# Two low parts of the first attention tile and one norm factor's power, issued later

## Chip, core and metric

The kernel runs on one core of a Trainium2 chip. The metric is device time in microseconds of one execution. Before the change three runs gave 1406.76, 1407.80 and 1407.81 us; the median is 1407.8.

## What is computed

The reference is one encoder block on a sequence of 1024 tokens of width 1024, with 16 meta tokens ahead of them. Two attention branches work on the same normalised input; their outputs are gated and merged, and a feed-forward block follows. The change is in branch A, which is differential attention:

```python
s1 = einsum(q1, k1) * scale + bias
s2 = einsum(q2, k2) * scale + bias
attn = softmax(s1) - lam * softmax(s2)
y = rms_norm(attn @ v, subln_g) * (1 - lambda_init)
...
merged = sigmoid(ga) * (y_a @ w_ba) + sigmoid(gb) * (y_b @ w_bb)
```

`ga` and `gb` are the gate projections of the input. All products are in fp32 precision: each factor is split into a high part (rounded to fp32r) and a low part (what the rounding left), and three fp32r products are added.

## The kernel before

Branch A has 4 heads of 8 tiles of 128 queries. For a tile, `scores_a` (line 1070 on) runs through the two softmaxes, m = 1 and then m = 0. For each, TensorE writes the first 704 keys to a double PSUM bank `two`, of which there is one, and the last 336 keys to a bank of the tag `sc`, of which there are three (line 1091). VectorE adds the bias and finds the row's extreme with one instruction for each part, lines 1094 and 1098; since signs are turned, it is a minimum, `amn`. Each is followed by a short instruction that reads the minimum out, and line 1098 starts from the minimum of line 1094. ScalarE takes the exponential and its sum (line 1102). After m = 0, VectorE works out the factor of the two sums (1107) and combines both softmaxes (1108, the "combine", 1040 columns).

One tile later, `transpose_a` turns the combined tile on TensorE in three blocks of 4, 4 and 1 pieces (line 1121), each into a bank `sc`. For each block ScalarE writes the high part (1124) and VectorE the low part (1125) to the tile `at`, which the value products (1134) read after two tiles.

After four tiles, `normed_a` makes the norm factors `af`: sums on TensorE (1147), a small VectorE step (1152), and on GpSimd a power of -1/2 on 128x4 numbers (1153). Some steps later TensorE spreads the factor (1158).

The products of branch A leave VectorE and ScalarE much to do, so the gate projections run in between on TensorE: `gate_steps` issues them in quarters of three products each (line 980). They use a Strassen scheme, so GpSimd first adds and subtracts weight blocks (lines 857, 858, 864 and others), then writes the high part (876, a cast) and the low part (877) of a gate weight `wopg`. Four of these exist at a time. A quarter's first two products need the high part, the third the low part.

The order on TensorE is the order of the code, set by the lists `SLOTS`, and GpSimd's is so at the start of branch A. On the other engines and queues a scheduler sets the order at build time from a simulated timeline; `tc.issue_after(x)` keeps what is issued under it behind instruction x. Each engine then works through its list in order.

Of the kernel before, what the change touches and what calls it, by code (L numbers as in the profile page):

```python
# [14 lines left out]
ALU = mybir.AluOpType  # L15
# [64 lines left out]
def encoder_block(ctx: ExitStack, tc: tile.TileContext, x, meta, norm_mix, w_in, lq1, lk1, lq2, lk2,  # L80
                  subln, sink, w_ba, w_bb, w_o, norm_ffn, w_g, w_u, w_d, norm_final, out, dbg=None):
    nc = tc.nc
# [5 lines left out]
    def f32(ap):  # L88
        return ap.bitcast(F32)
# [13 lines left out]
    def bank(p, tag, name, bufs):  # L103
        return p.tile([P, 512], F32, tag=tag, name=name, bufs=bufs)
# [15 lines left out]
    neg_half = const.tile([P, 4], F32, name="neg_half")  # L120
# [67 lines left out]
    def pp_bank(name):  # L188
        i = turn_pp[0] % 3
        turn_pp[0] += 1  # L190
        return bank(psum1, "pp", name, 1) if i == 2 else bank(psumg, f"pp{i}", name, 1)
# [339 lines left out]
    def turn_x(t, lows=None):  # L531
        parts = P if t < NT else NM
        return transposed(lambda name: bank(psum1, ("bt", "bs")[t % 2], name, 2), xns.pop(t), parts, hT_hi, hT_lo, t * P, f"a{t}", lows)
# [23 lines left out]
    pt = bank(psum1, "bt", "gain_t", 2)  # L557
# [3 lines left out]
    for b in range(2):  # L561
        pt = pp_bank(f"gain_{b}")
        gain.append(pt)
        for c in range(4):
            k = 4 * b + c
# [18 lines left out]
    low = normals[-1]  # L584
    for i in (0, 2, 1, 3):
        with tc.issue_after(low.ins):
            low = lows[i]()
# [28 lines left out]
    third, low, turned = turn_x(2)  # L616
# [5 lines left out]
    highs, low, turned = turn_x(3)  # L622
# [26 lines left out]
    _, low, _ = turn_x(NT)  # L649
# [189 lines left out]
    sums_g, keys_a, raws_g, values_in, turned_t, made_g = {}, [], [], [], {}, []  # L839
# [198 lines left out]
    def far_copy(n):  # L1038
        if n < AH * NT:
            with ExitStack() as after:  # L1040
                if n > 2:
                    after.enter_context(tc.issue_after(made_g[-1].ins))
                nc.gpsimd.tensor_copy(far_m[n % 3][:, 0:S - 704], dist[:, 1600 - n % NT * P:1600 - n % NT * P + S - 704])
# [30 lines left out]
    def scores_a(h, t, ld, s):  # L1074
        slope = 2.0 ** -(2 * (h + 1))
        qs, ks, _ = ld
        nm = f"{h}_{t}"
        mn = small.tile([P, 2, 4], F32, tag="amn", name=f"amn_{nm}")
        dn = small.tile([P, 2], F32, tag="adn", name=f"adn_{nm}")
        if t % 4 == 0:  # L1080
            sum_a[h, t // 4] = small.tile([P, 4], F32, tag="asum", name=f"asum_{nm}")
        first_sum = sum_a[h, t // 4][:, t % 4:t % 4 + 1]
        u0 = 896 - t * P
        far = far_m[(h * NT + t) % 3]
        for m in (1, 0):
            s[m] = s0s[t % 2] if m == 0 else apool.tile([P, L], F32, tag="s1", name=f"as1_{nm}", bufs=S_BUFS[1])
            two = psum2.tile([P, 2, 512], F32, tag="two", name=f"aps2_{nm}_{m}", bufs=1)
            for i, (k0, n) in enumerate(A_CHUNKS):
                ps = two[:, i] if i < 2 else bank(psum2, "sc", f"aps_{nm}_{m}", SC)
                for vv in range(2):  # L1090
                    nc.tensor.matmul(ps[:, :n], qs[m][:, t * P:(t + 1) * P], ks[m][:, vv, k0:k0 + n],  # L1091
                                     start=(vv == 0), stop=(vv == 1))
                if i == 1:
                    nc.vector.tensor_tensor_reduce(s[m][:, 0:2 * n].rearrange("p (a k) -> p a k", a=2), two[:, :, :n],  # L1094
                                                   dist[:, u0:u0 + 2 * n].rearrange("p (a k) -> p a k", a=2), slope, far_a,
                                                   ALU.add, ALU.min, mn[:, m, 0:1])
                elif i == 2:
                    nc.vector.tensor_tensor_reduce(s[m][:, k0:k0 + n], ps[:, :n], far, slope, mn[:, m, 0:1],  # L1098
                                                   ALU.add, ALU.min, mn[:, m, 1:2])
                if i < 2:  # L1100
                    yield
            nc.scalar.activation(s[m][:, 0:L], s[m][:, 0:L], AF.Exp, bias=mn[:, m, 1:2], scale=-1.0,  # L1102
                                 accum_out=dn[:, 1:2] if m else first_sum)
            if m:
                nc.vector.reciprocal(dn[:, 1:2], dn[:, 1:2])
            yield
        nc.vector.tensor_scalar(dn[:, 0:1], first_sum, dn[:, 1:2], neglam, ALU.mult, ALU.mult)
        nc.vector.scalar_tensor_tensor(s[0][:, 0:L], s[1][:, 0:L], dn[:, 0:1], s[0][:, 0:L], ALU.mult, ALU.add)
        more, last = s[0][:, L:L + 2 * NM].rearrange("p (a k) -> p a k", a=2), s[0][:, S:L].unsqueeze(1).broadcast_to([P, 2, NM])
        nc.scalar.copy(more, last)  # L1110
        far_copy(h * NT + t + 2)

    def transpose_a(h, t, s, at_):
        i = t % 2
        for b in range(3):
            nb = 4 if b < 2 else 1
            kp = P
            pt = bank(psum2, "sc", f"apt_{h}_{t}_{b}", SC).rearrange("p (k t) -> p k t", k=4)
            for j in range(nb):
                k = 4 * b + j  # L1120
                nc.tensor.transpose(pt[:kp, j, :], s[:, k * P:k * P + kp], ident)  # L1121
            hi = at_[:kp, 4 * b:4 * b + nb, 0, i * P:(i + 1) * P]
            lo = at_[:, 4 * b:4 * b + nb, 1, i * P:(i + 1) * P] if b < 2 else hi[:NM]
            nc.scalar.activation(hi, pt[:kp, :nb], AF.Copy)
            nc.vector.tensor_tensor(lo, pt[:lo.shape[0], :nb], f32(hi)[:lo.shape[0]], ALU.subtract)
            yield

    def values_a(h, t, v, at_, py):
# [9 lines left out]
    def normed_a(h, c, py):  # L1138
        nm = f"{h}_{c}"
        ysq = gwork.tile([P, 512], F32, tag="ysq", name=f"ysq_{nm}", bufs=1)  # L1140
        nc.scalar.activation(ysq, py, AF.Square)
        yg = ustage.tile([P, 512], F32, tag="yg", name=f"yg_{nm}", bufs=2)
        nc.scalar.activation(yg, py, AF.Copy, scale=gsub)
        yield
        pst = bank(psum2, "sc", f"apst_{nm}", SC)
        for i in range(4):
            nc.tensor.matmul(pst[:, i:i + 1], ysq[:, i * P:(i + 1) * P], ones, start=True, stop=True)
        f = small.tile([P, 4], F32, tag="af", name=f"af_{nm}", bufs=2)
        sums = sum_a.pop((h, c))
        e = small.tile([P, 4], F32, tag="ae", name=f"ae_{nm}", bufs=2)  # L1150
        nc.vector.scalar_tensor_tensor(e, sums, EPS, sums, ALU.mult, ALU.mult)
        nc.vector.scalar_tensor_tensor(f, pst[:, 0:4], 1.0 / P, e, ALU.mult, ALU.add)
        nc.gpsimd.tensor_tensor(f, f, neg_half, ALU.pow)
        for _ in range(N_WAIT):
            yield
        pf = bank(psum2, "sc", f"apf_{nm}", SC)
        for i in range(4):
            nc.tensor.transpose(pf[:, i * P:(i + 1) * P], f[:, i:i + 1].broadcast_to([P, P]), ident)
        nc.vector.tensor_tensor(yg, yg, pf, ALU.mult)
        nc.sync.dma_start(ya_d[h][:, c * 512:c * 512 + 512], yg)  # L1160
        yield
# [14 lines left out]
    def turn(done):  # L1176
        h, t, s, at_, v = done
        yield from transpose_a(h, t, s[0], at_)

    def later(done):  # L1180
        h, t, s, at_, v = done
        if t % 4 == 1:
            acc[0] = bank(psum2, "acc", f"apy_{h}_{t}", 1)
        yield from values_a(h, t, v, at_, acc[0])
        if (h, t) == (AH - 1, NT - 1):
            valued.append(t)
        if t % 4 == 3:
            yield from normed_a(h, t // 4, acc[0])
# [11 lines left out]
    for n in range(AH * NT + T_LAG):  # L1200
# [3 lines left out]
        if n < AH * NT:  # L1204
            h, t = divmod(n, NT)
# [23 lines left out]
            s = [None, None]  # L1229
# [382 lines left out]
    xns, sums_t, held = {}, {}, {}  # L1612
# [315 lines left out]
    for n in range(nf, len(steps)):  # L1928
        p, j = steps[n][1]
# [6 lines left out]
        if p in LOADS:  # L1936
            at, half, col = LOADS[p]
            if at <= j < at + 4:
                t, cols = 4 * half + j - at, slice(col * 512, col * 512 + 512)
# [63 lines left out]
```

## Time and profile before

| | |
|---|---|
| profiled execution | 1407.06 us |
| its span | 1405.3 us |
| TensorE busy | 1395.5 us, 99% |
| VectorE busy | 926.8 us, 66% |
| ScalarE busy | 682.2 us, 49% |
| GpSimd busy | 661.9 us, 47% |
| stretch 288 to 300 us | TensorE busy 11.58 of 12.00 us |
| stretch 384 to 394 us | TensorE busy 9.69 of 10.00 us |

A row of the timeline gives the start in us from the beginning of the span, the duration in us, the engine (PE is TensorE, DVE VectorE, ACT ScalarE, POOL GpSimd), the line, the operation, the tiles written and read, shapes and a count of merged instructions; in brackets stands the engine's idle time ahead of it and what ended it. A matmul's row is longer than its share of TensorE's time, since the next one starts before it ends; the distance between starts counts. A row of the list of waits gives total us, number of times and the longest.

### The profile page before, as it was taken

The numbers are of one execution on the slowest core, as the hardware profiler recorded it, in microseconds if no ns is written. First come the engines' busy times: TensorE is split into PE (matmuls) and PEld (weight loads), VectorE is DVE, ScalarE is ACT, GpSimd is POOL, SyncE is SP. The second block draws the span as 40 slices with busy tenths as digits, with TensorE's granted clock in tenths as the row PEclk, the third lists the DMA queues.
The fourth block names the chain that finished last, engine by engine and source line by source line (L and its number), as shares of the span: only waits on it lengthen the run. The fifth ranks groups of instructions, "written<-read, shape, count | busy, mean of one in ns | idle before, by whom it ended". The sixth has DMA issues, their size and how long they took to land.

```text
span 1405.3 us, 20672 instructions
## 1 busy us (share of the span) xinstructions
PE 1395.5 (99%) x7169; PEld 1199.8 (85%) x7169; DVE 926.8 (66%) x1594; ACT 682.2 (49%) x1322; POOL 661.9 (47%) x637
## 2 busy tenths in 40 slices
PE   9999999999999999999999999999999999999998
PEld 8989999988888989888888888888888888888886
DVE  7556667676677878657868965644455543887566
ACT  6355565555454656645446644333333333444454
POOL 5347884485686767613404154554455451000442
PEclk9999999999999999999999999999999999999999
DMA  8435658464896363485603534333323324954343
GB/s 235 102 93 169 206 190 285 130 203 137 276 301 219 109 208 106 164 300 165 225 16 140 168 120 146 116 113 113 99 97 112 105 98 135 335 183 142 121 127 143
DMA packets 188601, 226.56 MB, mean 161 GB/s; under 512 B 14584, under 2 KB 122048, under 8 KB 188368
## 3 DMA queue, kind: packets, MB, share of 16 engines
q1 hardware_dynamic: 184736, 219.79, 48.6%
q10 hardware_dynamic: 3760, 5.45, 1.2%
q8 instruction: 57, 0.93, 0.3%
q14 instruction: 48, 0.39, 0.1%
HBM read 152.48 MB, written 68.39 MB: 157 GB/s over the span
## 4 chain that ended last, share of the span: by engine, by line
PE 98%; DVE 1%; ACT 1%; POOL 0%; DMA 0%; issue 0%; ACTq 0%; DVEq 0%; POOLq 0%
PE pg L1765 30%; PE pd L1870 15%; PE pg L980 11%; PE ppa L790 6%; PE aps L1091 4%; PE po L1668 4%; PE apy L1134 3%; PE pp_ka L259 3%; PE pp_va L259 3%; PE pp_qb L259 3%; PE apt L1121 2%; PE bps L449 2%; PE pp_qa L259 2%; PE po L1676 2%; PE bpy L496 1%; PE bpt L490 1%
## 5 line engine op out<-in xcount | busy, mean ns | idle before, releaser
L1765 PE MATMUL pg<-t,wop 128*128 128x512 f32 x1056 | 242.4, 389 | 0.0
L1765 PEld LDWEIGHTS pg<-t,wop 128*128 128x128 f32 x1056 | 198.3, 188 | 41.1
L126 POOL TENSOR_TENSOR wop<-wf,wop 128x512 fp32r<-128x512 f32 x114 | 152.9, 1341 | 162.6 <-ACT wop L125 152.6
L1870 PE MATMUL pd<-ob,oa 128*128 128x512 f32 x924 | 209.6, 389 | 0.0
L1870 PEld LDWEIGHTS pd<-ob,oa 128*128 128x128 f32 x924 | 173.3, 188 | 36.1 <-DVE ob L126 0.2
L1765 PE MATMUL pg<-b,wop 128*128 128x512 f32 x792 | 183.3, 389 | 0.0
L980 PE MATMUL pg<-hT_hi,wopg 128*128 128x512 f32 x488 | 182.1, 400 | 0.3 <-POOL wopg L877 0.3
L1765 PEld LDWEIGHTS pg<-b,wop 128*128 128x128 f32 x792 | 148.5, 188 | 30.7
L125 ACT ACTIVATE wop<-wf 128x512 fp32r<-128x512 f32 x128 | 80.7, 632 | 72.7 <-PE pg L1765 47.7
L126 POOL TENSOR_TENSOR oa<-ra,oa 128x512 fp32r<-128x512 f32 x27 | 35.0, 1296 | 168.6 <-ACT oa L125 167.2
L1102 ACT ACTIVATE as<-as,amn 128x1040 f32<-128x1040 f32 x64 | 74.6, 1166 | 79.9 <-DVE amn L1098 78.6
L980 PEld LDWEIGHTS pg<-hT_hi,wopg 128*128 128x128 f32 x488 | 91.6, 188 | 14.9 <-POOL wopg L877 0.7
L125 ACT ACTIVATE oa<-ra 128x512 fp32r<-128x512 f32 x77 | 48.7, 632 | 108.2 <-PE pd L1870 46.4
L980 PE MATMUL pg<-hT_lo,wopg 128*128 128x512 f32 x244 | 95.8, 393 | 0.0
L1542 DVE TENSOR_TENSOR s<-wf,wf 128x512 f32<-128x512 f32 x22 | 17.4, 793 | 111.2 <-DMA wf<-in_w_ff_up_dram 69.7
L1091 PE MATMUL aps<-ak,aq 128*128 128x352 f32 (+1 forms) x384 | 86.3, 333 | 0.4 <-DVE amn L1094 0.4
L1094 DVE CUSTOM_DVE_ANT_0 as<-aps,dist,far_a 128x704 f32<-128x704 f32 x64 | 60.3, 943 | 20.5 <-PE aps L1091 20.4
L461 POOL TENSOR_SCALAR bs<-bs,bdn 128x432 f32<-128x432 f32 (+1 forms) x64 | 37.1, 599 | 74.9 <-DVE bdn L459 65.4
L1091 PEld LDWEIGHTS aps<-ak,aq 128*128 128x128 f32 x384 | 63.6, 189 | 7.6 <-DVE amn L1094 0.6
L451 DVE CUSTOM_DVE_ANT_0 bs<-bps,tbx,nsink 128x432 f32<-128x432 f32 (+1 forms) x64 | 38.1, 625 | 46.6 <-PE bps L449 24.8
L1792 ACT COPY p<-pg 128x512 f32<-128x512 f32 x44 | 25.9, 588 | 66.4 <-PE pg L1765 64.3
L1134 PEld LDWEIGHTS apy<-at,av 128*128 128x128 f32 x400 | 54.0, 189 | 4.1
(341 smaller groups left out, 3145.7 us busy)
## 6 DMA issues: line engine op xcount, KB each, us to landing
ra<-aop SPq DMA_DIRECT2D x77, 256.0 KB, 2.7
wf<-in_w_ff_gate_dram SPq DMA_DIRECT2D x25, 512.0 KB, 3.8
wf<-in_w_ff_up_dram SPq DMA_DIRECT2D x25, 512.0 KB, 3.7
aop<-as SPq DMA_DIRECT2D x40, 256.0 KB, 2.0
wg_s<-in_w_in_dram SPq DMA_DIRECT2D x18, 512.0 KB, 4.7
ak<-ka_d SPq DMA_DIRECT2D x16, 520.0 KB, 6.5
t_d<-tst SPq DMA_DIRECT2D x16, 512.0 KB, 4.1
wg_f<-in_w_in_dram SPq DMA_DIRECT2D x16, 512.0 KB, 5.2
```

The lines of the kernel that those rows point to most:

```text
L125: high = nc.scalar.activation(hi, src, AF.Copy)
L126: lo_eng.tensor_tensor(lo, src, f32(hi), ALU.subtract)
L259: product = nc.tensor.matmul(ps[:, :n], a[:, c, :], b[:, c, at:at + n], start=(u == 0), stop=(u == 3 * DC - 1))
L790: nc.tensor.matmul(ps, w[:, a, j, :], src(j, b, tk), start=(j == 0 and n == 0), stop=(j == 3 and n == 2))
L980: product = nc.tensor.matmul(ps, op[:, x, c, :], h[:, 4 * d + c, HALF[t]], start=(p in (1, 6, 7) and c == 0 and i == 0), stop=(p in (2, 6, ...
L1091: nc.tensor.matmul(ps[:, :n], qs[m][:, t * P:(t + 1) * P], ks[m][:, vv, k0:k0 + n], start=(vv == 0), stop=(vv == 1))
L1094: nc.vector.tensor_tensor_reduce(s[m][:, 0:2 * n].rearrange("p (a k) -> p a k", a=2), two[:, :, :n], dist[:, u0:u0 + 2 * n].rearrange("p ( ...
L1102: nc.scalar.activation(s[m][:, 0:L], s[m][:, 0:L], AF.Exp, bias=mn[:, m, 1:2], scale=-1.0, accum_out=dn[:, 1:2] if m else first_sum)
L1134: nc.tensor.matmul(py[:, cols], v[:kp, a, k, :], at_[:kp, k, b, :], start=(k == 0 and j == 0), stop=(k == 8))
L1668: nc.tensor.matmul(sets_o[p][u], oa[:, a, u * P:(u + 1) * P], ob[:, b, :], start=(p in (1, 5) and j == 0 and k == 0), stop=(p in (2, 3) an ...
L1765: nc.tensor.matmul(ps, op[:, x, c, :], b[:, y, c, :], start=(p in (1, 5) and c == 0 and n == 0), stop=(p in (4, 2, 3) and c == 3 and n == ...
L1870: nc.tensor.matmul(ps[u], oa[:, a, u * P:(u + 1) * P], ob[:, b, :], start=(p in (1, 2, 5) and j == 0 and k == 0), stop=(p in (2, 3, 4) and ...
```

## The change

In the first tile (head 0, tile 0) the low parts of blocks 0 and 2 are not issued in `transpose_a` but put into a list; the next instruction of line 1094 is followed by all that the list holds. Block 1 and all other tiles stay. For the second group of four tiles of head 0, the power is kept behind the last but one gate weight made so far.

```diff
@@ scores_a
                 if i == 1:
-                    nc.vector.tensor_tensor_reduce(s[m][:, 0:2 * n].rearrange("p (a k) -> p a k", a=2), two[:, :, :n],
+                    least = nc.vector.tensor_tensor_reduce(s[m][:, 0:2 * n].rearrange("p (a k) -> p a k", a=2), two[:, :, :n],
                                                    dist[:, u0:u0 + 2 * n].rearrange("p (a k) -> p a k", a=2), slope, far_a,
                                                    ALU.add, ALU.min, mn[:, m, 0:1])
+                    with tc.issue_after(least.ins):
+                        while held:
+                            held.pop()()
...
+    held = []
+
@@ transpose_a
-            nc.vector.tensor_tensor(lo, pt[:lo.shape[0], :nb], f32(hi)[:lo.shape[0]], ALU.subtract)
+            def low(lo=lo, of=pt[:lo.shape[0], :nb], hi=f32(hi)[:lo.shape[0]]):
+                return nc.vector.tensor_tensor(lo, of, hi, ALU.subtract)
+            if not h and not t and b != 1:
+                held.append(low)
+            else:
+                low()
@@ normed_a
-        nc.gpsimd.tensor_tensor(f, f, neg_half, ALU.pow)
+        with tc.issue_after(made_g[-2].ins) if (h, c) == (0, 1) else ExitStack():
+            nc.gpsimd.tensor_tensor(f, f, neg_half, ALU.pow)
```

TensorE and ScalarE issue the same rows in the same order as before. On VectorE two rows move, both near the start of branch A. In the names, `apt_0_0`, `apt_0_1` and `apt_0_2` are the three turned blocks of tile 0, `aps_0_1_0` are the first 704 scores of tile 1 with m = 0, and `aps_0_2_1` those of tile 2 with m = 1. "ISA" is the fused step of lines 1094 and 1098 or the reading of its minimum. This is VectorE before:

```order
L1105 RECIPROCAL adn_1_3592<-adn_1_3592 128x1
L1125 TENSOR_TENSOR at_0_3522<-apt_0_0_3628,at_0_3522 128x4x128
L1094 ISA as_1_3425,amn_1_3591<-aps_0_1_0_3635,dist,far_a 128x704
L1094 ISA amn_1_3591 128x1
L1098 ISA as_1_3425,amn_1_3591<-aps_1_0_3644,far_m_3421,amn_1_3591 128x336
L1098 ISA amn_1_3591 128x1
L1005 TENSOR_TENSOR p_2_3615<-pg_6_3624,p_2_3615 128x512
L1107 TENSOR_SCALAR adn_1_3592<-asum_0_3525,adn_1_3592,neglam 128x1
L1108 SCALAR_TENSOR_TENSOR as_1_3425<-as_0_1_3593,adn_1_3592,as_1_3425 128x1040
L1125 TENSOR_TENSOR at_0_3522<-apt_0_1_3657,at_0_3522 128x4x128
L1125 TENSOR_TENSOR at_0_3522<-apt_0_2_3672,at_0_3522 16x128
L1094 ISA as_0_2_3683,amn_2_3681<-aps_0_2_1_3684,dist,far_a 128x704
```

And this is the same place on VectorE in the changed kernel, where the low parts stand in line 1131, the combine in line 1111 and the second minima in line 1101:

```order
L1094 ISA as_1_3425,amn_1_3591<-aps_0_1_0_3634,dist,far_a 128x704
L1094 ISA amn_1_3591 128x1
L1131 TENSOR_TENSOR at_0_3522<-apt_0_0_3628,at_0_3522 128x4x128
L1101 ISA as_1_3425,amn_1_3591<-aps_1_0_3644,far_m_3421,amn_1_3591 128x336
L1101 ISA amn_1_3591 128x1
L1005 TENSOR_TENSOR p_2_3615<-pg_6_3624,p_2_3615 128x512
L1110 TENSOR_SCALAR adn_1_3592<-asum_0_3525,adn_1_3592,neglam 128x1
L1111 SCALAR_TENSOR_TENSOR as_1_3425<-as_0_1_3593,adn_1_3592,as_1_3425 128x1040
L1131 TENSOR_TENSOR at_0_3522<-apt_0_1_3657,at_0_3522 128x4x128
L1094 ISA as_0_2_3682,amn_2_3680<-aps_0_2_1_3683,dist,far_a 128x704
L1094 ISA amn_2_3680 128x1
L1131 TENSOR_TENSOR at_0_3522<-apt_0_2_3672,at_0_3522 16x128
```

Block 0 now stands behind the first minima of tile 1, m = 0, and ahead of the second ones; block 2 stands behind the first minima of tile 2, m = 1.

On GpSimd one row moves, where head 1 has begun and the factor `af` of the last four tiles of head 0 is made. `wopg_6` and `wopg_2` are the gate weights made there. Before:

```order
L858 TENSOR_TENSOR wg_f_1_4442<-wg_f_1_4442,wg_f_0_4440 128x512
L1153 TENSOR_TENSOR af_1_4629<-af_1_4629,neg_half 128x4
L876 CAST wopg_6_4575<-wg_f_1_4442 128x512
L877 TENSOR_TENSOR wopg_6_4575<-wg_f_1_4442,wopg_6_4575 128x512
L876 CAST wopg_2_4615<-wg_f_0_4440 128x512
L877 TENSOR_TENSOR wopg_2_4615<-wg_f_0_4440,wopg_2_4615 128x512
```

And GpSimd in the changed kernel:

```order
L858 TENSOR_TENSOR wg_f_1_4442<-wg_f_1_4442,wg_f_0_4440 128x512
L876 CAST wopg_6_4575<-wg_f_1_4442 128x512
L877 TENSOR_TENSOR wopg_6_4575<-wg_f_1_4442,wopg_6_4575 128x512
L876 CAST wopg_2_4615<-wg_f_0_4440 128x512
L1164 TENSOR_TENSOR af_1_4629<-af_1_4629,neg_half 128x4
L877 TENSOR_TENSOR wopg_2_4615<-wg_f_0_4440,wopg_2_4615 128x512
```

The power passes a whole gate weight and the high part of the next. On the queue of SyncE, which issues the transfers, one load of a gate weight (`wg_s`, line 836) goes behind one more piece of the turned input (`hT_lo`, line 906), and four stores of a query block alternate between high and low part.

## Prediction

> **What bounds the kernel now.** I read the page first, for the share of each engine.
>
> ```profile
> span 1405.3 us, 20672 instructions
> ...
> PE 1395.5 (99%) x7169; PEld 1199.8 (85%) x7169; DVE 926.8 (66%) x1594; ACT 682.2 (49%) x1322; POOL 661.9 (47%) x637
> ```
>
> TensorE is busy for 99% of the span, and the diff leaves its 3047 rows in the same order. So nothing that the change does to VectorE or GpSimd counts unless a TensorE wait begins, ends or changes length. Next I read the waits of TensorE alone; the number after the colon is the total in us.
>
> ```profile
> PE idle L556 <- DVE zeros L548: 1.2, 1, 1.2
> PE aps L1091 <- DVE amn L1094: 0.4, 1, 0.4
> PE pg L980 <- POOL wopg L877: 0.3, 1, 0.3
> PE ptn_a L169 <- DVE xn_a L156: 0.3, 1, 0.3
> ```
>
> The list has one row more, of the start-up like the first and the last here. The other two are one wait each in branch A, and the two halves of the change stand just ahead of them. The waits are counted from the modelled end of a matmul, so they understate the loss; I take the loss from the starts in the timeline.
>
> **Edit 1, the two low parts of the first tile.** First TensorE around its wait, in the order of the timeline.
>
> ```profile
> 289.45 0.60 PE L1121 MATMUL apt<-ident,as 128*128 128x128 f32 x4
> 289.81 0.89 PE L1091 MATMUL aps<-ak,aq 128*128 128x352 f32 x4
> ...
> 296.98 0.40 PE L980 MATMUL pg<-hT_hi,wopg 128*128 128x512 f32 x1
> 297.40 0.66 PE L1121 MATMUL apt<-ident,as 128*128 128x128 f32 x4
> 298.46 0.92 PE L1091 MATMUL aps<-ak,aq 128*128 128x352 f32 x4 [0.40 <-DVE amn L1094]
> ```
>
> Without a wait, scores follow a group of four transposes after 0.36 us (289.45 to 289.81), and a transpose follows a gate product after 0.23 (the step from 387.99 to 388.22, quoted further down). Here the transposes begin 0.42 after 296.98, which is 0.19 late, and the scores 1.06 after the transposes, which is 0.70 late. The whole loss is 0.89 us. Now VectorE, which releases both.
>
> ```profile
> 291.23 0.69 DVE L1125 TENSOR_TENSOR at<-apt,at 128x512 fp32r<-128x512 f32 x1 [0.81 <-ACT at L1124]
> 291.84 0.94 DVE L1094 CUSTOM_DVE_ANT_0 as<-aps,dist,far_a 128x704 f32<-128x704 f32 x1
> ...
> 292.94 0.57 DVE L1098 CUSTOM_DVE_ANT_0 as<-aps,far_m,amn 128x336 f32<-128x336 f32 x1
> ...
> 294.84 0.27 DVE L1107 TENSOR_SCALAR adn<-asum,adn,neglam 128x1 f32<-128x1 f32 x1 [0.72 <-ACT as L1102]
> 295.14 1.60 DVE L1108 SCALAR_TENSOR_TENSOR as<-as,adn,as 128x1040 f32<-128x1040 f32 x1
> 296.67 0.87 DVE L1125 TENSOR_TENSOR at<-apt,at 128x512 fp32r<-128x512 f32 x2
> 297.47 0.93 DVE L1094 CUSTOM_DVE_ANT_0 as<-aps,dist,far_a 128x704 f32<-128x704 f32 x1
> ...
> 299.41 0.95 DVE L1094 CUSTOM_DVE_ANT_0 as<-aps,dist,far_a 128x704 f32<-128x704 f32 x1 [0.26 <-PE aps L1091]
> ...
> 300.29 0.69 DVE L1125 TENSOR_TENSOR at<-apt,at 128x512 fp32r<-128x512 f32 x1
> 300.89 0.56 DVE L1098 CUSTOM_DVE_ANT_0 as<-aps,far_m,amn 128x336 f32<-128x336 f32 x1
> ```
>
> The row at 296.67 holds the low parts of blocks 1 and 2. The change puts block 2 behind the minima at 297.47. A large low part takes 0.60 of VectorE's time (300.29 to 300.89), so block 2 had 297.47 - 296.67 - 0.60 = **0.20 us**, and the scores of tile 2, for which TensorE waits, come free 0.20 earlier. This part is nearly sure. The low part itself is then done about 298.4, which delays nobody: the product that wants its PSUM bank next stands behind the scores of 298.46 and three gate products in TensorE's order.
>
> Block 0, the row at 291.23, goes behind the minima at 291.84. Those then wait for their scores alone. The scores of 289.81 end at 290.70, and in the row at 299.41 minima start 0.03 after such an end (298.46 + 0.92 = 299.38), so they start at 290.74 instead of 291.84. The low part fills the pause between reading the minimum and using it: the rows at 299.41, 300.29 and 300.89 are that very sequence, and the second minima begin 1.48 after the first. That gives 292.22 instead of 292.94, **0.72 us earlier**. The exponential on ScalarE follows the second minima, and line 1107 follows it.
>
> ```profile
> 293.55 1.17 ACT L1102 ACTIVATE as<-as,amn 128x1040 f32<-128x1040 f32 x1 [2.35 <-DVE amn L1098]
> ```
>
> It had waited 2.35 us for them, so it moves by the same 0.72, and the combine at line 1108 asks to start at 295.14 - 0.72 = 294.42. What it meets there is GpSimd.
>
> ```profile
> 292.99 1.29 POOL L857 TENSOR_TENSOR wg_f<-wg_f 128x512 f32<-128x512 f32 x1 [0.98 <-DMA wg_f<-in_w_in_dram]
> 294.36 1.29 POOL L858 TENSOR_TENSOR wg_f<-wg_f,wg_f 128x512 f32<-128x512 f32 x1
> ...
> 303.21 1.29 POOL L857 TENSOR_TENSOR wg_f<-wg_f 128x512 f32<-128x512 f32 x1
> ```
>
> A combine with free road takes 1.30 us. The one at 295.14 took 1.60: it began while the GpSimd addition of 294.36 ran to 295.65, and got on 0.21 before that row's end, at 295.44. The later combine tells the same.
>
> ```profile
> 303.15 2.45 DVE L1108 SCALAR_TENSOR_TENSOR as<-as,adn,as 128x1040 f32<-128x1040 f32 x1
> ```
>
> Its work began at 303.15 + 2.45 - 1.30 = 304.30, again 0.20 before the end of the GpSimd row (303.21 + 1.29 = 304.50), although it had asked 0.06 before that row's start. So the earlier request of 294.42 comes 0.06 us after the addition of 294.36 has started, waits to 295.44 as before, and **the 0.72 are lost in that wait**. The Trainium skill, page "SBUF — State Buffer", section "Who interferes with whom", says that a VectorE instruction with two SBUF inputs contends with a GpSimd instruction that reads SBUF, and that the one issued first keeps the shared pair for the whole instruction. By that rule the gain of this edit stays at 0.20, and by durations alone, with no such lock, it would be 0.89. The rows at 295.14 and 303.15 agree with the rule on who waits, but show the release 0.2 before the recorded end.
>
> The two ends for this edit are therefore 0.20 (combine behind the addition) and 0.89 (combine ahead of it). I take 0.20, because the request is 0.06 on that side; but 0.06 is little, and the addition hangs on a weight from DRAM (the 0.98 at 292.99), so the other end has a large chance.
>
> **Edit 2, the power.** GpSimd first, then TensorE.
>
> ```profile
> 380.37 1.30 POOL L858 TENSOR_TENSOR wg_f<-wg_f,wg_f 128x512 f32<-128x512 f32 x1
> 384.86 2.08 POOL L1153 TENSOR_TENSOR af<-af,neg_half 128x4 f32<-128x4 f32 x1 [3.19 <-DVE af L1152]
> 386.90 0.61 POOL L876 CAST wopg<-wg_f 128x512 fp32r<-128x512 f32 x1
> 387.58 1.29 POOL L877 TENSOR_TENSOR wopg<-wg_f,wopg 128x512 fp32r<-128x512 f32 x1
> ...
> 389.50 1.29 POOL L877 TENSOR_TENSOR wopg<-wg_f,wopg 128x512 fp32r<-128x512 f32 x1
> ```
>
> ```profile
> 387.99 0.39 PE L980 MATMUL pg<-hT_hi,wopg 128*128 128x512 f32 x1
> 388.22 0.40 PE L980 MATMUL pg<-hT_lo,wopg 128*128 128x512 f32 x1
> 388.92 0.73 PE L980 MATMUL pg<-hT_hi,wopg 128*128 128x512 f32 x2 [0.31 <-POOL wopg L877]
> 389.49 0.40 PE L980 MATMUL pg<-hT_lo,wopg 128*128 128x512 f32 x1
> ...
> 393.44 0.60 PE L1158 MATMUL apf<-ident,af 128*128 128x128 f32 x4
> ```
>
> The power waits 3.19 us for its input and takes 2.08, and the gate weight behind it ends at 387.58 + 1.29 = 388.87, just before TensorE goes on at 388.92. Due was 388.22 + 0.23 = 388.45, so 0.47 is lost; the next two products take 0.57 instead of 0.46, another 0.10. Together **0.57 us**. In the change the weight's cast and subtraction fill GpSimd's idle time from 381.67: 0.07 + 0.61 + 0.07 + 1.29 makes the weight ready at 383.7, then the cast of the next weight runs to 384.4, and the power finds its input at the same 384.86 as now. Behind the power stands the second half of that next weight, done at 384.86 + 2.08 + 0.05 + 1.29 = 388.3 against 389.50 + 1.29 = 390.8 now. The power ends at 386.94 and its own reader on TensorE stands at 393.44, so 6.5 us cover it. If the next cast were late by more than 0.46, the power would be late by the excess, and that cover would still swallow it.
>
> Two exchanges on the queue of SyncE go with this: a weight load one place later, behind a piece of `hT_lo`, and two stores in turn. The row of that piece is this one.
>
> ```profile
> 398.97 0.42 SPq L906 DMA_DIRECT2D hT_lo<-t_d  x1
> ```
>
> The load is issued some 0.42 us later. On TensorE that is worth between 0 and 0.42; I take 0, since GpSimd, which reads that weight, has 9 us of idle time soon after (the row at 424.95 below).
>
> **The sum.** 0.20 + 0.57 = 0.77 us. The profiled execution took 1407.06 for its span of 1405.3; less 0.77 is **1406.3**. The median of the three runs shown is 0.74 above the profiled one, the lowest 0.30 below, so the spread of runs is as large as the effect.
>
> **Rivals.** (1) *The combine gets in first.* If the weight lands over 0.06 us later, the combine starts at 294.42 and ends at 295.72, the low part of block 1 at 296.3, and both stalls around 297 vanish: 0.89 + 0.57 = 1.46, hence 1405.6. For it: the start hangs on a DMA. Against it: the order in this trace. (2) *Half of it comes to nothing*, since another wait takes a removed one's place, or a transfer that lands late: a gain of 0 to 0.57, 1406.5 to 1407.1. For it: the transposes of 297.40 wait for the low part of block 1, which the forecast leaves where it is. Against it: the list of waits has no third row after the start-up, so little else stands close. (3) *The lead of GpSimd shifts its collisions onto tight tiles*, and the kernel is slower. In the second half of branch A minima end shortly before TensorE needs the bank.
>
> ```profile
> 450.27 0.93 DVE L1094 CUSTOM_DVE_ANT_0 as<-aps,dist,far_a 128x704 f32<-128x704 f32 x1
> ```
>
> ```profile
> 451.52 0.81 PE L1091 MATMUL aps<-ak,aq 128*128 128x352 f32 x4
> ```
>
> That slack is 451.52 - 451.20 = 0.32 us, and a newly met addition costs the combine up to 1.29 - 0.21 = 1.08, so up to 0.76 on TensorE each time. One such hit makes up for the forecast gain (1407.1); from the second on the kernel is slower, and five make it 1410.1. Against it stands this row.
>
> ```profile
> 424.95 1.02 POOL L1153 TENSOR_TENSOR af<-af,neg_half 128x4 f32<-128x4 f32 x1 [9.07 <-DVE af L1152]
> ```
>
> GpSimd waits here 9.07 us for a factor that comes from TensorE's own progress. The lead of about 2.5 us (390.8 to 388.3) ends there, and the tight tiles see GpSimd where they see it now. The rival needs a lead of over 9 us.
>
> **How the numbers follow.** Forecast 50%, rival 1 32%, rival 2 11%, rival 3 7%. The range goes from 1405.1, rival 1 on a low run, to 1407.9, no gain on the highest run shown. About 0.2%, or 2.8 us, is what a measurement of this kernel can tell from no change. All but rival 3 lie within it, except rival 1 against a high run of before: faster 4%, same 92%, slower 4%.
>
> **What would show it.** TensorE's wait for the gate weight is gone from its list, and the power starts behind a cast. The wait for the minima stays with about half its length and its combine ends where it did, or, by rival 1, is gone with a combine of 1.30 us at 294.4. I am wrong if TensorE has a new wait after 300 us, or if the power's idle time moves in front of a weight that TensorE needs.

## The result and the profile after

The changed kernel takes 1405.54 us (median of 22 runs, 1404.68 to 1407.39), the kernel before 1407.66 (22 runs, 1406.76 to 1408.9). The ratio is 0.9984, 95% interval 0.9978 to 0.999: 2.1 us faster, by the interval 1.4 to 3.1. That is 0.16%, inside the 0.2% that the prediction called no telling difference, and inside its range; but the forecast gain was 0.77 us, so 1.35 us of it were not foreseen. The profiled execution of the changed kernel took 1405.57 us. This is the page's first part.

```profile
span 1403.6 us, 20673 instructions
...
PE 1395.2 (99%) x7169; PEld 1200.3 (86%) x7169; DVE 926.1 (66%) x1594; ACT 682.1 (49%) x1322; POOL 661.3 (47%) x637
```

No engine has clearly less to do. The waits of TensorE after the change:

```profile
PE idle L556 <- DVE zeros L548: 1.2, 1, 1.2
PE aps L1091 <- DMA ak<-ka_d: 0.4, 1, 0.4
PE gain L566 <- DVE columns L559: 0.3, 1, 0.3
```

Both waits that the change aimed at are gone, the one for the minima wholly and not by half. (The start-up wait `ptn_a` of before is missing too, but at 289 us TensorE stands only 0.10 us ahead of before.) In their place stands one that was not there: scores at 511.90 that wait for keys from DRAM.

```profile
511.22 0.32 PE L1091 MATMUL aps<-ak,aq 128*128 128x352 f32 x1
511.90 0.77 PE L1091 MATMUL aps<-ak,aq 128*128 128x352 f32 x3 [0.36 <-DMA ak<-ka_d]
```

Now the place of edit 1 in the changed kernel. VectorE first: the first minima, the low part of block 0, the second minima, the combine, the low part of block 1 and the minima of tile 2.

```profile
290.63 0.95 DVE L1094 CUSTOM_DVE_ANT_0 as<-aps,dist,far_a 128x704 f32<-128x704 f32 x1 [0.31 <-PE aps L1091]
...
291.51 0.69 DVE L1131 TENSOR_TENSOR at<-apt,at 128x512 fp32r<-128x512 f32 x1
292.11 0.56 DVE L1101 CUSTOM_DVE_ANT_0 as<-aps,far_m,amn 128x336 f32<-128x336 f32 x1
...
294.31 1.53 DVE L1111 SCALAR_TENSOR_TENSOR as<-as,adn,as 128x1040 f32<-128x1040 f32 x1
295.76 0.68 DVE L1131 TENSOR_TENSOR at<-apt,at 128x512 fp32r<-128x512 f32 x1
296.36 0.93 DVE L1094 CUSTOM_DVE_ANT_0 as<-aps,dist,far_a 128x704 f32<-128x704 f32 x1
```

GpSimd beside it, with the two additions of the weight:

```profile
293.45 1.29 POOL L857 TENSOR_TENSOR wg_f<-wg_f 128x512 f32<-128x512 f32 x1 [2.59 <-DMA wg_f<-in_w_in_dram]
294.82 2.18 POOL L858 TENSOR_TENSOR wg_f<-wg_f,wg_f 128x512 f32<-128x512 f32 x1
```

The weight landed late here: its first addition starts at 293.45 and not at 292.99. So the combine, which asks at 294.31, met the end of that one (293.45 + 1.29 = 294.74), waited 1.53 - 1.30 = 0.23 and was through at 295.84. The addition that the forecast put ahead of it asked at 294.82 and was the one that waited: 2.18 instead of 1.29. TensorE then runs without a gap, 0.23 from gate product to transposes and 0.35 on to the scores.

```profile
296.89 0.40 PE L980 MATMUL pg<-hT_hi,wopg 128*128 128x512 f32 x1
297.12 0.60 PE L1126 MATMUL apt<-ident,as 128*128 128x128 f32 x4
297.47 0.89 PE L1091 MATMUL aps<-ak,aq 128*128 128x352 f32 x4
```

At the place of edit 2 GpSimd has the power (line 1164) behind a cast, and the low part that TensorE needs is ready at 382.69:

```profile
381.39 1.30 POOL L877 TENSOR_TENSOR wopg<-wg_f,wopg 128x512 fp32r<-128x512 f32 x1
382.64 0.61 POOL L876 CAST wopg<-wg_f 128x512 fp32r<-128x512 f32 x1
383.84 2.08 POOL L1164 TENSOR_TENSOR af<-af,neg_half 128x4 f32<-128x4 f32 x1 [0.60 <-DVE af L1162]
385.89 1.30 POOL L877 TENSOR_TENSOR wopg<-wg_f,wopg 128x512 fp32r<-128x512 f32 x1
```

TensorE takes it without a wait, 0.23 from start to start and 0.47 over the next two products:

```profile
387.20 0.39 PE L980 MATMUL pg<-hT_lo,wopg 128*128 128x512 f32 x1
387.43 0.63 PE L980 MATMUL pg<-hT_hi,wopg 128*128 128x512 f32 x2
387.90 0.39 PE L980 MATMUL pg<-hT_lo,wopg 128*128 128x512 f32 x1
```

Set start against start of the same matmul in the two traces, TensorE gains 0.19 us at the transposes (0.42 to 0.23), 0.71 from there to the scores (1.06 to 0.35), 0.57 at the gate weight, and gives back 0.64 at 511.90 and at the product behind it. With the 0.10 it was ahead and smaller drifts, its last product ends at 1397.29 and not at 1398.28. The difference is 1.0 us, but the span is 1.6 us shorter: what follows the last product has become shorter too, from 6.98 to 6.36 us.

### The profile page after: what moved, and what is told of

Read it like the earlier page. It is cut to its first block, busy times and chain, and to the rows that moved or that the text cites. A ratio compares the mean times of both kernels' runs of the same rounds, so it can differ in the third digit from the quotient of the medians.

```text
span 1403.6 us, 20673 instructions
## 1 busy us (share of the span) xinstructions
PE 1395.2 (99%) x7169; PEld 1200.3 (86%) x7169; DVE 926.1 (66%) x1594; ACT 682.1 (49%) x1322; POOL 661.3 (47%) x637
## 4 chain that ended last, share of the span: by engine, by line
PE 98%; DMA 1%; DVE 0%; ACT 0%; issue 0%; SPq 0%; ACTq 0%; DVEq 0%
PE pg L1776 30%; PE pd L1881 15%; PE pg L980 11%; PE ppa L790 6%; PE aps L1091 4%; PE po L1679 4%; PE pp_ka L259 3%; PE pp_va L259 3%; PE apy L1144 3%; PE pp_qb L259 3%; PE apt L1126 2%; PE bps L449 2%; PE pp_qa L259 2%; PE po L1687 2%; PE bpy L496 1%; PE bpt L490 1%
```

## Experiments

All were timed in 11 runs each beside the kernel before. One interval is about 0.0009 of the time to each side (1.3 us), more than most single effects; so the profiles decide, and the medians are used together. "Loss at the scores" is what TensorE's starts at the transposes and scores around 297 us are late, by the prediction's measure (steps of 0.23 and 0.36 are free).

| run | median us | ratio to before [95%] | loss at the scores | behind the last product |
|---|---|---|---|---|
| before, first profile | 1407.66 | | 0.89 | 6.98 |
| b_again | 1407.46 | 1.0001 [0.9992, 1.001] | 1.31 | 6.99 |
| lows_only | 1406.67 | 0.9996 [0.9987, 1.0005] | 0 | 6.98 |
| power_only | 1406.22 | 0.9991 [0.9982, 1.0] | 1.19 | 6.36 |
| block0_only | 1407.18 | 0.9995 [0.9987, 1.0004] | 0.88 | 6.98 |
| block2_only | 1407.52 | 0.9997 [0.9989, 1.0006] | 0.95 | 6.98 |
| a_again | 1405.51 | 0.9988 [0.9979, 0.9997] | 0.62 | 6.36 |
| combine_first | 1406.61 | 0.9994 [0.9985, 1.0003] | 0.58 | 6.17 |
| power_act1 | 1406.48 | 0.9992 [0.9984, 1.0001] | 0.71 | 6.35 |
| after_dve1 | 1406.19 | 0.9989 [0.9981, 0.9998] | 0 | 6.98 |
| before_dve1 | 1406.74 | 0.9995 [0.9986, 1.0004] | 1.14 | 6.19 |
| after_hold | 1406.01 | 0.9989 [0.9981, 0.9998] | 0 | 6.98 |
| after_hold_dve1 | 1405.40 | 0.9984 [0.9975, 0.9993] | 0 | 6.17 |

### The same kernels once more

**b_again** is the kernel before, **a_again** the changed one, both unaltered; they show how far one profile can be trusted.

> The kernel before, unchanged, as a measure of what a run shows by chance. Theory V (the 2.1 us of the change are 1.46 us of TensorE's waits plus what varies from run to run behind them): ratio 1.000 within 0.0005, and TensorE's loss at the scores of tile 2 is 0.89 us as in the first profile. Theory L (the weight from DRAM lands later in most runs than the 292.9 us of the first profile of before, so that the combine of tile 1 waits longer): ratio also 1.000, but the weight's addition of line 857 starts nearer to 293.5 us, the combine of line 1108 ends up to 0.5 us later, and the loss there is 1.0 to 1.4 us.

> The changed kernel once more. Theory L with F: ratio near 0.9985 (1.2 to 1.3 us at the low parts, 0.57 at the gate weight, 0.62 at the end), the end takes 6.36 us, and the wait of 0.64 us for head 3's keys at 512 us, which the first profile of it had and that of before had not, comes and goes by chance.

b_again, GpSimd, VectorE and TensorE:

```profile
294.69 1.29 POOL L858 TENSOR_TENSOR wg_f<-wg_f,wg_f 128x512 f32<-128x512 f32 x1
```

```profile
295.06 2.03 DVE L1108 SCALAR_TENSOR_TENSOR as<-as,adn,as 128x1040 f32<-128x1040 f32 x1
```

```profile
296.90 0.39 PE L980 MATMUL pg<-hT_hi,wopg 128*128 128x512 f32 x1
297.75 0.66 PE L1121 MATMUL apt<-ident,as 128*128 128x128 f32 x4 [0.45 <-DVE at L1125]
298.80 0.43 PE L1091 MATMUL aps<-ak,aq 128*128 128x352 f32 x1 [0.40 <-DVE amn L1094]
```

The addition started 0.33 later than in the first profile, so the same combine waited longer (2.03 instead of 1.60), and TensorE lost 0.85 - 0.23 = 0.62 at the transposes and 1.05 - 0.36 = 0.69 at the scores: 1.31 us, not 0.89. The loss that the prediction started from hangs on when a weight lands; its first addition started at 293.32 here, so Theory L of the expectation held. In a_again the weight landed early:

```profile
294.27 1.30 POOL L858 TENSOR_TENSOR wg_f<-wg_f,wg_f 128x512 f32<-128x512 f32 x1
```

```profile
294.40 2.26 DVE L1111 SCALAR_TENSOR_TENSOR as<-as,adn,as 128x1040 f32<-128x1040 f32 x1
```

```profile
296.97 0.40 PE L980 MATMUL pg<-hT_hi,wopg 128*128 128x512 f32 x1
297.32 0.66 PE L1126 MATMUL apt<-ident,as 128*128 128x128 f32 x4
298.18 0.91 PE L1091 MATMUL aps<-ak,aq 128*128 128x352 f32 x4 [0.21 <-DVE amn L1094]
```

This is the forecast as written: the combine asks 0.13 behind the start of the addition, waits to 0.21 before its end (294.40 + 2.26 - 1.30 = 295.36 against 295.57), and TensorE's scores come 0.86 behind the transposes instead of 1.06, the 0.20 of the forecast, with half of the wait left. (The transposes are 0.07 better as well; the first addition of this weight started 0.11 earlier than in the first profile of before.) One and the same kernel shows the forecast in one profile and rival 1 in the other.

### Each half alone, and each block alone

**lows_only** has the part of the diff in `scores_a` and `transpose_a`, **power_only** the last two lines of the diff. **block0_only** and **block2_only** are lows_only with one block put off:

```diff
-            if not h and not t and b != 1:
+            if not h and not t and b == 0:
```

```diff
-            if not h and not t and b != 1:
+            if not h and not t and b == 2:
```

> The two low parts moved, the power left where it was. My forecast (combine behind the GpSimd addition): 0.20 us faster. Theory V: combine ahead of it, 0.9 us faster (ratio 0.9994), and the wait for the gate weight at 388 us is still there. Theory L: 0.9 to 1.5 us faster (ratio 0.9989 to 0.9994), above 0.9 in the median, with no loss left at the scores of tile 2.

> The power moved (with it the two exchanges on SyncE's queue), the low parts left. Theories V and L and the forecast agree on the place: the wait for the gate weight at 388 us gone, 0.57 us faster (ratio 0.9996), the loss at the scores of tile 2 as in before. A rival: the exchanges on the queue matter too, and the gain is over 1 us; then some other TensorE wait of before would be missing.

> Only block 0's low part moved; block 2's stands again between the combine and the minima of tile 2. The combine asks to start 0.72 us earlier. Theory L: it gets in ahead of the GpSimd addition (line 858), takes 1.30 to 1.55 us and TensorE's loss at the scores of tile 2 is 0 to 0.1 us, as with both low parts moved; ratio near 0.9993. My forecast (the 0.72 are lost behind the addition) would leave a loss of 0.9 to 1.3 us there and a ratio of 1.000.

> Only block 2's low part moved. It tells the two low parts apart: by my working the combine and all ahead of it stay where they are and the minima of tile 2 start 0.20 us earlier, so TensorE's loss there is 0.20 us smaller than in the kernel before with the same landing of the weight: ratio 0.9999, not to be told from 1 by time. If instead the loss goes by 0.5 us or more, the first block's move is not what frees the combine.

In lows_only the combine was first (294.37, against 294.52 of the addition) and took 1.30; the loss of TensorE was gone. The wait for the gate weight stayed, as the step of 0.71 in place of 0.23 on TensorE shows:

```profile
387.21 0.40 PE L980 MATMUL pg<-hT_lo,wopg 128*128 128x512 f32 x1
387.92 0.72 PE L980 MATMUL pg<-hT_hi,wopg 128*128 128x512 f32 x2 [0.31 <-POOL wopg L877]
```

In power_only that wait was gone, 0.57 us as worked out. Its median stands 1.4 us under that of the before runs beside it; by the interval that is 0 to 2.5, so the time alone can't tell it from 0.57. But in its trace what follows the last product took 6.36 us, as in the changed kernel; in lows_only it took 6.98, as before. So the surplus comes with the power, and it lies at the end.

block2_only has 0.87 from transposes to scores instead of 1.06, so 0.19 of the forecast's 0.20; its weight landed late, and its transposes lost 0.26 more than in the first profile of before. block0_only, GpSimd, VectorE and TensorE:

```profile
293.85 1.29 POOL L858 TENSOR_TENSOR wg_f<-wg_f,wg_f 128x512 f32<-128x512 f32 x1
```

```profile
293.91 2.32 DVE L1111 SCALAR_TENSOR_TENSOR as<-as,adn,as 128x1040 f32<-128x1040 f32 x1
```

```profile
296.48 0.40 PE L980 MATMUL pg<-hT_hi,wopg 128*128 128x512 f32 x1
296.89 0.66 PE L1126 MATMUL apt<-ident,as 128*128 128x128 f32 x4
297.95 0.91 PE L1091 MATMUL aps<-ak,aq 128*128 128x352 f32 x4 [0.41 <-DVE amn L1094]
```

The combine asked at 293.91, 1.23 us earlier than before (295.14). The run stood 0.50 ahead there (the gate product at 296.48 against 296.98), which leaves 0.73 for the moved low part. It came 0.06 us behind the addition, and TensorE's steps are those of before within a hundredth (0.41 and 1.06, against 0.42 and 1.06). That is the forecast's clause on block 0 in its pure form; the expectation by Theory L, the combine ahead and at most 0.1 us lost, was missed, since this weight landed earliest of all (292.47). Over 11 runs its times go from 1405.80 to 1407.80 us, which fits a step that comes out one way or the other; that the lowest are those with the combine ahead is argued, not shown, since only one run has a profile.

### Is it the addition that the combine waits for?

**combine_first** is the kernel before, with the additions of that weight held on GpSimd behind a one-column copy that reads the combine's result. `weights_after` is `weights_g` of before under a new name; the second part leaves out the request that would make this weight (n = 8) ahead of the combine, so that the next request makes it:

```diff
+        if n == 8:
+            seen = nc.gpsimd.tensor_copy(room[:, 0:1], s0s[1][:, 0:1])
+            with tc.issue_after(seen.ins):
+                weights_after(n)
...
-            ensure_g(n + 4)
+            if n != 5:
+                ensure_g(n + 4)
```

> The kernel before with all its low parts where they were; instead GpSimd's work on the gate weight of lines 857 and 858 is held until the combine of tile 1 has ended (a one-column copy on GpSimd reads its result first). Theory of the shared wait: the combine starts at 295.1 us as before but takes 1.30 instead of 1.6 to 2.0, so the minima of tile 2 end 0.3 to 0.7 us earlier and TensorE's loss there falls from about 1.3 to about 0.6 us; the gate weight is ready at about 301.5, before the 303.9 at which TensorE wants it. If the combine still takes 1.6 or more, it was not the additions that held it.

GpSimd, VectorE and TensorE:

```profile
296.40 0.19 POOL L844 COPY room<-as 128x1 f32<-128x1 f32 x1 [5.57 <-DVE as L1118]
296.54 1.29 POOL L866 TENSOR_TENSOR wg_f<-wg_f 128x512 f32<-128x512 f32 x1
```

```profile
295.04 1.30 DVE L1118 SCALAR_TENSOR_TENSOR as<-as,adn,as 128x1040 f32<-128x1040 f32 x1
```

```profile
297.11 0.60 PE L1131 MATMUL apt<-ident,as 128*128 128x128 f32 x4
298.05 0.91 PE L1101 MATMUL aps<-ak,aq 128*128 128x352 f32 x4 [0.34 <-DVE amn L1104]
```

Without an addition beside it the combine takes 1.30, the transposes are no longer late, and the loss is 0.58 instead of 1.31 in b_again, where the combine asked within 0.02 us of this. So of b_again's loss 0.7 us were the wait for the additions, and 0.6 are VectorE's own order, which the moved low parts mend (after_hold below has no loss left).

### What is shorter behind the last product?

Of the trace's two DMA queues for instructions, q14 is the one that matters here. One 8192-byte packet of it lies 4.61 us behind the end of TensorE's last product in before, among the last output stores, and 6.66 us behind it in after, when they have landed. The last store lands 6.14 us behind that product in before and 5.23 in after. The trace tells each store's landing in 16 parts: in before 15 of them are in by 5.23, as in after, and a single one comes at 6.14; of the store ahead of it 15 are in by 4.99 and one comes at 5.96. VectorE's list in the trace, with the entries that only wait, has 2114 entries before and 2113 after; power_only has 2113, lows_only 2114. Three theories: the packet is VectorE's and comes when its list reaches a fixed place; it is another engine's; or the exchanges on SyncE's queue do it.

**power_act1** is power_only with one more column copied by ScalarE at the start. **after_dve1** and **before_dve1** are the changed kernel and the kernel before with one more one-column VectorE instruction, issued far from the places of the change:

```diff
-        nc.vector.scalar_tensor_tensor(e, sums, EPS, sums, ALU.mult, ALU.mult)
+        small_e = nc.vector.scalar_tensor_tensor(e, sums, EPS, sums, ALU.mult, ALU.mult)
+        if (h, c) == (1, 1):
+            with tc.issue_after(small_e.ins):
+                for i in range(1):
+                    nc.vector.memset(room[:, 8 + i:9 + i], 0.0)
```

> The power moved, and one tiny copy of one column added on ScalarE at the very start. In the runs so far the kernels with the power moved end 6.36 us after the last product and the others 6.98, and an instruction fetch falls 4.6 us behind the last product in the others, among the last stores, and 6.7 us behind it with the power moved. Theory F (the fetch is ScalarE's, whose list became one instruction shorter): the fetch is back at 4.6 us, the end takes 6.98 us again, and the gain over the kernel before is only the 0.57 us at the gate weight: ratio 0.9996 to 0.9997. Theory Q (the exchanged transfers on SyncE's queue shorten the end) or a fetch of another engine: the end stays 6.36 us, ratio 0.9991 as with the power alone.

> The changed kernel with one tiny memset of one column added on VectorE in the middle of branch A, far from both places of the change; no other row moves on any engine. Theory F, now with VectorE as the owner of the fetch (its list had 2114 entries in the trace before and 2113 in the change): the list is as long as before again, the fetch falls 4.6 us behind the last product, the end takes 6.98 us, and the kernel loses about 0.6 us against the change: ratio about 0.9991. Theory Q (the exchanged transfers shorten the end): the end stays 6.36 us, ratio as the change.

> The kernel before with the same tiny memset and nothing else. Theory F: VectorE's list grows by one, the fetch comes earlier than 4.6 us behind the last product (a kernel whose list had 2115 entries had it at 2.3 us), and if it misses the last stores, the end takes 6.2 to 6.4 us instead of 6.98: ratio 0.9994 to 0.9996 with every TensorE wait of before in place. Theory Q: the end stays 6.98, ratio 1.000.

These are the DMA rates in GB/s, 40 slices of 0.15 us from some 1.7 us behind the last product on, of before, after, after_dve1 and before_dve1:

```profile
GB/s 396 328 82 218 410 355 423 314 28 0 14 341 382 423 382 328 396 396 383 355 82 27 0 14 0 27 0 0 0 0 0 0 0 0 0 0 0 0 0 0
```

```profile
GB/s 396 328 96 205 410 369 396 328 41 0 14 328 396 423 382 355 382 410 383 328 96 0 0 0 0 0 0 0 0 0 0 0 55 0 0 0 0 0 0 0
```

```profile
GB/s 382 382 82 205 396 382 382 341 41 0 0 328 396 410 396 328 382 410 383 369 82 27 0 14 0 27 0 0 0 0 0 0 0 0 0 0 0 0 0 0
```

```profile
GB/s 396 396 164 123 396 396 355 369 110 0 27 259 369 382 396 410 396 355 383 396 178 14 0 0 0 0 0 0 0 0 0 0 0 0 0 0 0 0 0 0
```

In before the last stores have a thin rest of five slices (27, 0, 14, 0, 27), 0.75 us long. In after it is missing, and the packet stands alone in the slice with 55, behind everything. One VectorE instruction more brings the rest back (after_dve1: 6.98 us behind the last product). One more on the kernel before takes it away by the other road: the packet moves up to 2.35 us, where it delays an earlier pair of stores (landed 2.95 and 4.10 us behind the last product, against 2.54 and 3.40) that others still follow, and the end takes 6.19. ScalarE's extra copy does nothing: power_act1 has VectorE's 2113, the packet at 6.66 and 6.35 us. before_dve1 has no moved power and after_dve1 has it, so SyncE's exchanges are not the cause; nor are the lists of the other engines, which the moved power changes by one entry each (GpSimd 901 to 902, SyncE 1226 to 1227, ScalarE 1893 to 1892) and which after_dve1 has as in after. The medians agree in sign (after_dve1 0.7 us above after, before_dve1 0.7 us below the kernel before), but by their intervals they alone would not show it.

### The best of both

**after_hold** is the changed kernel with the hold of combine_first, **after_hold_dve1** this one with the VectorE instruction of after_dve1.

> The changed kernel with the hold of the combine_first run added: GpSimd's additions for that gate weight start behind the combine of tile 1, so their race is gone. Theory of the shared wait: the combine takes 1.30 us in every run, no loss at the scores of tile 2 (-0.19 and -0.64 against the first profile of before), the gate weight in time: at least as fast as the change's better runs on TensorE, 1.46 us less than the first profile of before up to the last product, and narrower in its spread. The end takes 6.2, 6.4 or 6.98 us as the fetch falls, which I can't foretell. If TensorE waits for the held gate weight, the kernel is slower than the change.

> The kernel after with the hold on GpSimd (its first addition of the weight behind the first tile's combine) and one more one-column VectorE instruction in branch A, so that VectorE's list in the trace has 2115 entries instead of the 2114 of the run with the hold alone. Theory F (the fetch of VectorE's next instructions falls at a place of the end that the length of its list sets): the 8192-byte packet lies about 2.3 us behind the last product, as in the two other kernels with 2115 entries, and the end behind the last product takes 6.17 to 6.2 us instead of 6.98; with the combine at 1.30 us ahead of the additions and the power's 0.57 us kept, 1405.1 to 1405.4 us. Theory N (the end differs for another reason than the length of VectorE's list, for instance by which weight loads stand where): the end stays at 6.98 us and the time at 1406.0.

Both have the combine at 1.30 us ahead of the additions and all of TensorE's gains (no loss at the scores, 0.57 at the gate weight). after_hold has 2114 entries and 6.98 us behind the last product, after_hold_dve1 2115 and 6.17, with the packet at 2.33 us. In the same view of DMA rates, after_hold_dve1:

```profile
GB/s 410 328 69 232 396 369 410 273 55 14 27 355 396 410 410 341 382 396 396 341 96 0 0 0 0 0 0 0 0 0 0 0 0 0 0 0 0 0 0 0
```

The expectation of the place and of the end was met. At 1405.40 us it is the lowest median, but not one that can be told from the 1405.54 of the changed kernel: in its profile TensorE gives back 0.35 us at 501.87 (below) and 0.8 between 1198 and 1205 us, where the chain of waits names loads from DRAM and the other profiles lose 0.3 at most.

## Why the prediction was right and wrong

**Block 2, "0.20 us": right.** a_again and block2_only show 0.20 and 0.19.

**Block 0, "0.72 us earlier": right.** The second minima start 1.48 behind the first (290.63 to 292.11), and the combine asks at 294.31, forecast at 294.42, in a run that stood 0.10 ahead there.

**"The 0.72 are lost in that wait": the step that failed as a choice.** The mechanism held: whichever of combine and addition asks first holds the other up, until about 0.2 us before its row's end, as a_again and block0_only show. But which comes first was read off one landing of a weight. The first addition started between 292.47 (block0_only) and 294.05 us (power_act1) in the profiles where it was not held. After the change the combine was ahead in three profiles with both low parts moved (after, lows_only, after_dve1) and behind in one (a_again). By these four the rival at 32% was at least as frequent as the forecast at 50%.

**The size of that rival, "0.89": too small.** It, too, came from the one early landing. Of the five profiles with the low parts in their old place and no hold, the loss at the scores was 0.89, 1.31, 1.19, 1.14 and 0.71, on the mean 1.05. In the four with both moved and no hold it was 0, 0, 0 and 0.62, on the mean 0.16. The edit is worth about 0.9 us on the mean by these few profiles, up to 1.3 in one run.

**Edit 2, "0.57 us": right** in every profile with the power moved: 0.70 us from the first to the last of TensorE's rows shown above (387.20 to 387.90), where the others have 1.26 to 1.28 over the same products. The lead that GpSimd has from it ends where the prediction said, in the wait for the next factor:

```profile
423.31 1.02 POOL L1164 TENSOR_TENSOR af<-af,neg_half 128x4 f32<-128x4 f32 x1 [11.08 <-DVE af L1162]
```

**"Nothing that the change does to VectorE or GpSimd counts unless a TensorE wait begins, ends or changes length": wrong.** 0.62 us came from behind TensorE's last product. The sum had no term there; with the power moved, VectorE's list became one entry shorter, and a fetch of instructions left the last stores.

The terms together: 0.57 + 0.62 = 1.19, and with 0.20 to 1.31 for edit 1 it is 1.39 to 2.50, or 1.19 + 0.89 = 2.08 by the means. Measured were 2.12 and, in a_again, 1.95.

**The time: inside the range, in part by luck.** Rival 1's 1405.6 is almost the measured 1405.54, but not by its terms. It was taken off the profiled run, 1407.06, which lies 0.6 us below the median of before, and it has no term for the end, 0.62; the two nearly cancel. The range held the result because it reached down to rival 1 on a low run. The forecast's own gain, 0.77 us, was little more than a third of the measured one.

**"I am wrong if TensorE has a new wait after 300 us."** It had one at 511.90 in the profile of after, 0.64 us. a_again has a smaller one there (0.27), and so have block0_only (0.32) and block2_only (0.75), in which the power did not move; power_only, lows_only, after_dve1 and after_hold have none. So it is not the moved power's, and the same kernel has it longer or shorter from run to run. But all four profiles that have it have a moved low part (four of eight such profiles, none of the other six), so it isn't ruled out that the moved low parts make this wait more likely. What sets that landing was not tried.

## What to carry to other kernels

Where a gain hangs on which of two engines asks first and a DMA decides that, one profile gives one throw: take several profiles of the same kernel, and price the wait over the whole spread of the landing. Read the end behind the last product as a stage of its own, since a list that is one entry longer or shorter can move an instruction fetch into or out of the last stores. When a part gives more than its own wait could, compare where the last product ends with where the span ends before looking for hidden waits.

## What the runs showed of the hardware

**VectorE's instruction fetch beside the last stores.** In all 14 profiles the length of VectorE's list gives the end behind the last product: 2113 entries, packet at 6.66 to 6.67 us, end 6.35 to 6.36 (four profiles); 2114, 4.60 to 4.61 us, 6.98 to 6.99 (seven); 2115, 2.33 to 2.35 us, 6.17 to 6.19 (three). One entry moves the packet by 2.0 to 2.3 us. When it comes, 2111 to 2113 entries of VectorE's list have started in every profile, so its place counts from the list's start. With 2114 entries a single one of the 16 parts of each of the last two stores lands 0.9 to 1.0 us behind the others; with 2115 it is one part of the pair before, 0.4 and 0.7 us late; with 2113 none. Behind the last landing, after still takes 6.36 - 5.23 = 1.13 us where before takes 0.84; why was not tried.

**A place in VectorE's list that costs 0.35 us.** In the three kernels with 2115 entries, and in none of the others, VectorE pauses ahead of one instruction. This is before_dve1:

```profile
501.89 0.16 DVE L1105 RECIPROCAL adn<-adn 128x1 f32<-128x1 f32 x1
502.46 0.57 DVE L1098 CUSTOM_DVE_ANT_0 as<-aps,far_m,amn 128x336 f32<-128x336 f32 x1 [0.42 <-DVE adn L1105]
```

The pause is 0.42 instead of 0.07, and TensorE loses 0.35 at its next transposes. That instruction is the 960th entry of the list there, and the 958th or 959th in the others. In the other lists the 960th entry is another instruction and has no such pause. Whether the number is the reason was not tried by itself.
